# Feed-forward stages of a two-block layer stack on one core: one matmul of 512 columns for two of 256, a residual that is normalized once, and weight splits in halves

## Chip, cores, metric

One NeuronCore of a Trainium2 chip runs the whole program, in one launch. The metric is the device time in microseconds (us), from runs of the same program; lower is better.

## What is computed

Two small transformer blocks behind each other on one sequence of 256 tokens with 1024 channels, in fp32. The first block has a layer with stick-breaking and sparse attention and a layer with forgetting attention, each followed by a feed-forward part with a causal convolution of width 3; the second has a gated linear recurrence and a dilated attention, each with a plain feed-forward part before and behind it. So there are six feed-forward parts, each with 2816 hidden channels:

```python
def rmsnorm(x, g):
    y = x * lax.rsqrt(jnp.mean(x * x, axis=-1, keepdims=True) + NORM_EPS)
    return y * g

def conv_glu_ffn(h, w_in, conv_w, conv_b, w_out):       # first block, twice
    a, b = jnp.split(h @ w_in, 2, axis=-1)
    a = causal_depthwise_conv(a, conv_w) + conv_b
    return (jax.nn.silu(a) * b) @ w_out                 # x = x + that

def _swiglu(h, w_in, w_out):                            # second block, four times
    gate, up = jnp.split(h @ w_in, 2, axis=-1)
    return (jax.nn.silu(gate) * up) @ w_out             # x = x + 0.5 * that
```

with `h = rmsnorm(x, gain)`. Between the blocks the final norm of the first is applied to x, and the first norm of the second follows at once.

## The kernel before

The residual `x` lies transposed in SBUF, channels on the partitions: 8 chunks (KC) of 128 channels by 256 tokens (T). The matrices are products of fp32 numbers made of fp32r matmuls: each operand is split into a high part (`H`, rounded to fp32r) and a low part (`L`, the rest), and a product is three matmuls, H x H, H x L and L x H, added up in PSUM. TensorE (PE) holds 128x128 weights (a weight load, PEld in the trace, goes with each matmul) and streams 256 tokens.

*Weights.* `w` (L266 to L278) fetches a piece of 8 (or 6) chunks by 256 columns, 1 MB, by a DMA that SP issues, into one of two `raw` buffers, and `w_split` (L262 to L264) makes H on ACT (a copy, L263) and L on DVE (a subtraction, L264), by quarters of 512 columns. There are four buffers for the split pieces.

*The residual's operand.* When a chunk of x is final, `done` calls `split_x`: ACT writes xH = x * gain (L328), DVE writes xL = x * gain - xH (L329). The norm's factor R (one number for each token) is not in the operand; it is multiplied in behind the matmul.

*A feed-forward stage* is `ffn` (L447 to L519). `project` makes a piece of two blocks of 128 hidden channels with `gemm`, 48 matmuls (L308 to L310) into one PSUM bank; six banks go round. For m = 0, 2, ..., 20 there is one piece of gate and one of up. `norm` (or `first`, in the third stage) makes R while the first pieces run: squares on ACT, sums on DVE, a matmul with ones over the partitions, then Ln and Exp on ACT and a Newton step on DVE whose last operation is L401. `act` takes the two banks: DVE multiplies by R (L475 or L478 for the gate, L488 for up), the convolution runs on ACT and DVE (L481, L484), Silu on ACT, the product on DVE (L489), and `split` (L313, L314) writes it as hH and hL. The output part goes over four pairs of 128 channels, three weight pieces each; its matmuls (`mm3`, L282 to L284) go into two banks, one for each 128 channels, and one operation on DVE (L516, or L518 with the factor 0.5) adds each to x; then `done` follows.

*Third stage.* `first` makes the factor of the first block's final norm, R1, and from it that of the second block's first norm; it also rewrites x = x * gain * R1, eight operations on DVE (L1448). The product of both factors is what `act` multiplies by.

The order on each engine is set when the program is built, by a list scheduler that goes by priorities and its own estimates of durations; on the chip each engine works its list off in order and waits on semaphores. The stages in order: even (attention), f0, fox (attention), f1, s00, hgrn (recurrence), s01, s10, dilated (attention), s11. In the trace, f0 is the first feed-forward stage and s00 the third.

## Time and profile before

| | |
|---|---|
| median of 3 runs | 1888.78 us (1884.24 to 1891.77) |
| span of the profiled execution | 1880.8 us, 37768 instructions |
| time of that execution beside its span | not listed apart; the three times lie 3.4 to 11.0 us above the span |
| matmuls, weight loads | 15687 each |
| weights read | 311 MB from HBM, 166 GB/s over the span |
| granted clock of TensorE, mean | 0.999 |

The profile is of one execution. PE's busy time is made of modelled ends and counts a matmul from its start to its end, although they overlap; how close it is to its peak is seen from the distances of the starts. A group's line can be that of a helper: all matmuls of `gemm` stand at L308 to L310, whichever stage calls it. A unit of the split is told by its tile (`wH`, `xH`, `hH`).

### The profile page before, as it was taken

The numbers are of one execution on the slowest core, as the hardware profiler recorded it, in microseconds if no ns is written. First come the engines' busy times: TensorE is split into PE (matmuls) and PEld (weight loads), VectorE is DVE, ScalarE is ACT, GpSimd is POOL, SyncE is SP. The second block draws the span as 40 slices with busy tenths as digits, with TensorE's granted clock in tenths as the row PEclk, the third lists the DMA queues.
The fourth block names the chain that finished last, engine by engine and source line by source line (L and its number), as shares of the span: only waits on it lengthen the run. The fifth ranks groups of instructions, "written<-read, shape, count | busy, mean of one in ns | idle before, by whom it ended". The sixth has DMA issues, their size and how long they took to land.

```text
span 1880.8 us, 37768 instructions
## 1 busy us (share of the span) xinstructions
PE 1865.1 (99%) x15687; PEld 1830.0 (97%) x15687; DVE 1271.5 (68%) x2695; ACT 1041.1 (55%) x2167; POOL 3.9 (0%) x18
## 2 busy tenths in 40 slices
PE   8999999999999999999999999999999999999999
PEld 7989999999999999999999999999999999999999
DVE  6557886654888586658998765767566456558662
ACT  5456655455666455445766544645456556556442
POOL 0000000000000000000000000000000000000000
PEclk9999999999999999999999999999999999999999
DMA  7303555541555546455335555555554434326552
GB/s 250 124 32 135 207 196 180 183 152 57 182 218 201 186 165 216 175 185 180 118 107 209 198 192 181 197 185 191 186 204 159 154 130 152 123 90 221 185 195 96
DMA packets 61160, 314.72 MB, mean 167 GB/s; under 512 B 10459, under 2 KB 21115, under 8 KB 28348
## 3 DMA queue, kind: packets, MB, share of 16 engines
...
q8 instruction: 123, 2.02, 0.4%
...
HBM read 311.17 MB, written 1.11 MB: 166 GB/s over the span
## 4 chain that ended last, share of the span: by engine, by line
PE 96%; DVE 2%; DMA 1%; ACT 1%; issue 0%; SPq 0%; ACTq 0%
PE ps_mm L308 21%; PE ps_mm L310 21%; PE ps_mm L309 21%; PE ps_mm L284 7%; PE ps_mm L282 7%; PE ps_mm L283 7%; PE ps_S L317 5%; PE ps_o L317 4%; DMA raw<-in_wall_dram 1%; PE ps_PT L1340 1%; PE ps_PT L317 1%; PE ps_PT L588 1%; DVE wL L264 1%; PE ps_PT L1285 0%; PE ps_PT L614 0%; DVE x L535 0%
## 5 line engine op out<-in xcount | busy, mean ns | idle before, releaser
L263 ACT CAST wH<-raw 128x512 fp32r<-128x512 f32 (+1 forms) x1212 | 651.3, 597 | 525.1 <-PE ps_mm L309 259.9
L264 DVE TENSOR_TENSOR wL<-raw,wH 128x512 fp32r<-128x512 f32 (+1 forms) x1212 | 755.8, 662 | 260.5 <-ACT wH L263 256.8
L308 PE MATMUL ps_mm<-xH,wH 128*128 128x256 f32 x2560 | 717.2, 280 | 8.6 <-ACT xH L328 7.0
L310 PE MATMUL ps_mm<-xH,wL 128*128 128x256 f32 x2560 | 716.1, 280 | 0.2 <-DVE wL L264 0.2
L309 PE MATMUL ps_mm<-xL,wH 128*128 128x256 f32 x2560 | 714.8, 279 | 0.6 <-DVE xL L329 0.4
L308 PEld LDWEIGHTS ps_mm<-xH,wH 128*128 128x128 f32 x2560 | 484.7, 189 | 10.4 <-ACT xH L328 7.0
L309 PEld LDWEIGHTS ps_mm<-xL,wH 128*128 128x128 f32 x2560 | 483.7, 189 | 1.4 <-DVE xL L329 1.3
L310 PEld LDWEIGHTS ps_mm<-xH,wL 128*128 128x128 f32 x2560 | 482.7, 189 | 1.1 <-DVE wL L264 0.7
L284 PE MATMUL ps_mm<-hH,wL 128*128 128x256 f32 x1056 | 297.6, 282 | 0.0
L282 PE MATMUL ps_mm<-hH,wH 128*128 128x256 f32 x1056 | 297.6, 282 | 0.0
L283 PE MATMUL ps_mm<-hL,wH 128*128 128x256 f32 x1056 | 297.5, 282 | 0.0
L283 PEld LDWEIGHTS ps_mm<-hL,wH 128*128 128x128 f32 x1056 | 200.3, 190 | 0.0
L284 PEld LDWEIGHTS ps_mm<-hH,wL 128*128 128x128 f32 x1056 | 200.3, 190 | 0.0
L282 PEld LDWEIGHTS ps_mm<-hH,wH 128*128 128x128 f32 x1056 | 200.3, 190 | 0.0
L308 PE MATMUL ps_mm<-wH,kH 128*128 128x256 f32 x384 | 108.3, 282 | 0.0
L309 PE MATMUL ps_mm<-wL,kH 128*128 128x256 f32 x384 | 107.6, 280 | 0.0
L310 PE MATMUL ps_mm<-wH,kL 128*128 128x256 f32 x384 | 107.5, 280 | 0.0
L308 PE MATMUL ps_mm<-wH,xH 128*128 128x256 f32 x368 | 104.3, 284 | 0.0
L310 PE MATMUL ps_mm<-wH,xL 128*128 128x256 f32 x368 | 103.6, 282 | 0.0
L309 PE MATMUL ps_mm<-wL,xH 128*128 128x256 f32 x368 | 103.4, 281 | 0.0
L488 DVE TENSOR_TENSOR t<-ps_mm,R 128x512 f32<-128x512 f32 x66 | 45.5, 690 | 82.6 <-PE ps_mm L310 82.5
L308 PE MATMUL ps_mm<-oH,wH 128*128 128x256 f32 x256 | 73.4, 287 | 0.0
...
## 6 DMA issues: line engine op xcount, KB each, us to landing
...
```

Of the source, the lines that this page charges most:

```text
L263: self.nc.scalar.copy(H[:, s], raw[:, s])
L264: self.nc.vector.tensor_sub(L[:, s], raw[:, s], H[:, s].bitcast(F32))
L282: nc.tensor.matmul(out, A[0], B[0], start=start, stop=False)
L283: nc.tensor.matmul(out, A[0], B[1], start=False, stop=False)
L284: nc.tensor.matmul(out, A[1], B[0], start=False, stop=stop)
L308: nc.tensor.matmul(out[:, j, :], A[0], B[0], start=c == c0 and j == 0, stop=False, **k)
L309: nc.tensor.matmul(out[:, j, :], A[0], B[1], start=False, stop=False, **k)
L310: nc.tensor.matmul(out[:, j, :], A[1], B[0], start=False, stop=c == c1 - 1, **k)
L317: self.nc.tensor.matmul(out, l, r, start=start, stop=stop, **k)
L488: nc.vector.tensor_mul(t2[:], u, Rb)
L588: nc.tensor.transpose(pp[:, i * P:(i + 1) * P], s, self.ident[:])
L1340: nc.tensor.transpose(pp[:, i], Pt[:, t, i * P:(i + 1) * P], self.ident[:])
```

## The change

In the feed-forward stages alone:

- H and L of an operand lie in one tile (`xB`, `nB`, `hB`, and `wB` for the weights), so that one matmul can stream both: `pair_step` lets the high weights meet [H | L], 512 columns, into a whole bank, and then the low weights meet H, 256 columns, into its first half. Two matmuls and two weight loads where there were three. The sum lies in two halves of a bank, which are added when it is read (`join`: ACT copies the second half out, DVE adds the first; in the output part two additions to x).
- A piece takes two banks (one for each 128 channels), so three pieces share the six banks.
- The operand is normalized once: `normalize` makes nB = split(x * gain * R), two chunks at a time, after the norm. Only the pieces with m < 4 (`EARLY`) still use the raw operand and multiply by R behind it.
- Weight pieces of `nB` and of the output part are split in halves of 1024 columns instead of quarters.

All other changes are names (of tiles, and `gain` as an argument of `ffn`), places of small tiles and comments that are gone; their line numbers move by up to 49. The core of the diff:

```diff
 def w(self, *key):
...
-            for i in range(4):
-                self.w_split(raw, H, L, slice(i * n // 4, (i + 1) * n // 4))
+            q = self.parts
+            for i in range(q):
+                self.w_split(raw, H, L, slice(i * n // q, (i + 1) * n // q))
...
+    def pair(self):
+        t = self.ps.tile([P, 1024], F32, name="ps_pair", tag="pair", bufs=self.tags["pair"] // 2)
+        return t[:].rearrange("p (j h t) -> p j h t", j=2, h=2)
+
+    def pair_step(self, o, WH, WL, XB, first, last):
+        mm, k = self.nc.tensor.matmul, {"skip_group_check": True}
+        mm(o, WH, XB, start=first, stop=False, **k)
+        mm(o[:, 0, :], WL, XB[:, 0, :], start=False, stop=last, **k)
+
+    def gemm_pair(self, o, W, XB):
+        for c in range(KC):
+            for j in range(2):
+                s = slice(j * P, (j + 1) * P)
+                self.pair_step(o[:, j], W[0][:, c, s], W[1][:, c, s], XB[:, :, c, :], c == 0, c == KC - 1)
...
 def ffn(...):
+        EARLY = 4
-            self.banks(ctx, mm=6, sm=2)
+            self.banks(ctx, pair=6, sm=2)
...
             def project(m, n):
-                o = self.psum((P, 2, T))
-                W = self.w(tag, n, m)
-                self.gemm(o, W)
+                self.parts = 4 if m < EARLY else 2
+                o = self.pair()
+                self.gemm_pair(o, self.w(tag, n, m), self.xB if m < EARLY else nB)
+                self.parts = 4
                 return o
+            def normalize(c0, Rx):
+                t = fp.tile([P, 2, T], F32, name="xn", tag="t2")
+                for i in range(2):
+                    c = c0 + i
+                    nc.vector.scalar_tensor_tensor(t[:, i, :], self.x[:, c, :], gain[:, c:c + 1], Rx[:],
+                                                   op0=ALU.mult, op1=ALU.mult)
+                self.split(nB[:, 0, c0:c0 + 2, :], nB[:, 1, c0:c0 + 2, :], t[:])
+
+            def join(dst, o, tmp, early):
+                nc.scalar.copy(tmp, o[:, :, 1, :])
+                if early:
+                    nc.vector.tensor_add(tmp, o[:, :, 0, :], tmp)
+                    nc.vector.tensor_mul(dst, tmp, R[:, None, :].to_broadcast([P, 2, T]))
+                else:
+                    nc.vector.tensor_add(dst, o[:, :, 0, :], tmp)
...
-                    nc.vector.tensor_mul(t1[:], g, Rb)
+                    join(t1[:], g, t1[:], m < EARLY)
...
                 if m == 2:
                     act(0, g, u)
+                    for c in range(0, KC, 2):
+                        normalize(c, Rx)
...
-                            self.mm3(o[j], (W[0][:, c, s], W[1][:, c, s]), (hH[:, k, :], hL[:, k, :]),
-                                     k == 0, k == NF - 1)
+                            self.pair_step(o[:, j], W[0][:, c, s], W[1][:, c, s], hB[:, :, k, :], k == 0, k == NF - 1)
                 for j in range(2):
                     x = self.x[:, m + j, :]
-                    if alpha == 1.0:
-                        nc.vector.tensor_add(x, o[j], x)
+                    for h in (1, 0):
+                        if alpha == 1.0:
+                            nc.vector.tensor_add(x, o[:, j, h, :], x)
...
 def first():
...
-            R = self.sp.tile([P, T], F32, name="R12", bufs=1)
-            self.rsqrt_rows(R[:], m2[:])
-            nc_.vector.tensor_mul(R[:], R[:], R1[:])
+            R2 = self.hp.tile([P, T], F32, name="R2", bufs=1)
+            self.rsqrt_rows(R2[:], m2[:])
+            nc_.vector.tensor_mul(R[:], R2[:], R1[:])
...
-            return R
+            return R, R2
```

How the change moves instructions is seen at three places. The first is PE in stage s00, where the fourth piece ends and the fifth begins (the number behind a tile's name is that of its buffer). Before:

```order
L308 MATMUL ps_mm_8223<-xH_75,wH_8225 128x256
L309 MATMUL ps_mm_8223<-xL_76,wH_8225 128x256
L310 MATMUL ps_mm_8223<-xH_75,wL_8226 128x256
L308 MATMUL ps_mm_8292<-xH_75,wH_8294 128x256
L309 MATMUL ps_mm_8292<-xL_76,wH_8294 128x256
L310 MATMUL ps_mm_8292<-xH_75,wL_8295 128x256
```

and in the changed kernel:

```order
L325 MATMUL ps_pair_6897<-xB_75,wB_6898 128x256
L324 MATMUL ps_pair_6897<-xB_75,wB_6898 128x512
L325 MATMUL ps_pair_6897<-xB_75,wB_6898 128x256
L324 MATMUL ps_pair_6953<-nB_6659,wB_6954 128x512
L325 MATMUL ps_pair_6953<-nB_6659,wB_6954 128x256
L324 MATMUL ps_pair_6953<-nB_6659,wB_6954 128x512
```

Three rows have become two, and the operand changes from `xB` to `nB` at the fifth piece, where it stayed the same before.

The second is DVE in the same stage, from the end of the norm's factor on. Before (R12 is the product of both factors):

```order
L401 TENSOR_TENSOR R12_8137<-R12_8137,rsr_8138 128x256
L264 TENSOR_TENSOR wL_8425<-raw_8423,wH_8424 128x512
L1446 TENSOR_TENSOR R12_8137<-R12_8137,R_8120 128x256
L264 TENSOR_TENSOR wL_8425<-raw_8423,wH_8424 128x512
L475 TENSOR_TENSOR t1_8216<-ps_mm_7960,R12_8137 128x512
L488 TENSOR_TENSOR t2_8215<-ps_mm_8021,R12_8137 128x512
L475 TENSOR_TENSOR t1_8285<-ps_mm_8154,R12_8137 128x512
L488 TENSOR_TENSOR t2_8284<-ps_mm_8223,R12_8137 128x512
L264 TENSOR_TENSOR wL_8486<-raw_8484,wH_8485 128x512
L489 TENSOR_TENSOR t2_8215<-t2_8215,t1_8216 128x512
```

and in the changed kernel (R2 is the second factor alone, `xn` the normalized chunks):

```order
L422 TENSOR_TENSOR R2_6804<-R2_6804,rsr_6805 128x256
L266 TENSOR_TENSOR wB_7044<-raw_7045,wB_7044 128x1024
L1495 TENSOR_TENSOR R12_6803<-R2_6804,R_6786 128x256
L499 SCALAR_TENSOR_TENSOR xn_6877<-x_74,par_71,R2_6804 128x256
L508 TENSOR_TENSOR t1_6866<-t1_6866,R12_6803 128x512
L508 TENSOR_TENSOR t2_6865<-t2_6865,R12_6803 128x512
L499 SCALAR_TENSOR_TENSOR xn_6877<-x_74,par_71,R2_6804 128x256
L499 SCALAR_TENSOR_TENSOR xn_6882<-x_74,par_71,R2_6804 128x256 x2
L508 TENSOR_TENSOR t1_6942<-t1_6942,R12_6803 128x512
L530 TENSOR_TENSOR t2_6865<-t2_6865,t1_6866 128x512
L335 TENSOR_TENSOR nB_6659<-xn_6877,nB_6659 128x512
```

Between the factor and the first two chunks of `nB` (last row) stand one half of a weight split and the products of the early pieces.

The third is PE at the beginning of fox, where the norm's sum over the partitions stands among the first matmuls of that stage. Before:

```order
L310 MATMUL ps_mm_4167<-xH_75,wL_4170 128x256
L308 MATMUL ps_mm_4167<-xH_75,wH_4169 128x256
L309 MATMUL ps_mm_4167<-xL_76,wH_4169 128x256
L317 MATMUL ps_PT_4327<-acc_4314,ones_77 128x256
L310 MATMUL ps_mm_4167<-xH_75,wL_4170 128x256
```

and in the changed kernel:

```order
L312 MATMUL ps_mm_3517<-xB_75,wB_3518 128x256
L313 MATMUL ps_mm_3517<-xB_75,wB_3518 128x256
L311 MATMUL ps_mm_3517<-xB_75,wB_3518 128x256
L338 MATMUL ps_PT_3675<-acc_3662,ones_76 128x256
L312 MATMUL ps_mm_3517<-xB_75,wB_3518 128x256
```

The row with `acc` was the 27th behind the last output matmul of f0 and is now the 20th.

## Rows read from the trace of the kernel before

**Rows 1.** The page of the profile: its part 1 (busy us of each engine, share of the span, instructions) and the first lines of its part 4 (the chain of work that ended last, as shares of the span by engine, then by engine, tile and line).
```profile
PE 1865.1 (99%) x15687; PEld 1830.0 (97%) x15687; DVE 1271.5 (68%) x2695; ACT 1041.1 (55%) x2167; POOL 3.9 (0%) x18
...
PE 96%; DVE 2%; DMA 1%; ACT 1%; issue 0%; SPq 0%; ACTq 0%
...
PE ps_mm L308 21%; PE ps_mm L310 21%; PE ps_mm L309 21%; PE ps_mm L284 7%; PE ps_mm L282 7%; PE ps_mm L283 7%; PE ps_S L317 5%; PE ps_o L317 4%; DMA raw<-in_wall_dram 1%; PE ps_PT L1340 1%; PE ps_PT L317 1%; PE ps_PT L588 1%; DVE wL L264 1%; PE ps_PT L1285 0%; PE ps_PT L614 0%; DVE x L535 0%
```

**Rows 2.** The waits of PE, longest first: who waited <- for whom: us in total, times, longest.
```profile
PE ps_mm L308 <- ACT xH L328: 7.0, 1, 7.0
...
PE ps_PT L317 <- DVE acc L386: 0.5, 1, 0.5
```

**Rows 3.** The busy time of each engine by stretch, for the input and the output stretch of each of the six feed-forward stages (all six input stretches, two of the six output stretches, and the sum over all twelve). Columns: from:to, length, busy us and instructions of PE, PEld, DVE, ACT and POOL, granted clock, share of DMA, GB/s.
```profile
171.40:296.20 124.80, 124.80 (x1058) 124.75 (x1059) 105.09 (x191) 77.14 (x143) 0.00 (x0) 1.00 0.54 193
...
487.60:608.10 120.50, 120.50 (x1061) 120.45 (x1060) 106.00 (x193) 78.23 (x145) 0.17 (x3) 1.00 0.55 200
...
608.10:670.50 62.40, 62.40 (x530) 62.40 (x529) 36.00 (x65) 30.43 (x60) 0.00 (x0) 1.00 0.53 189
...
670.60:795.40 124.80, 124.80 (x1062) 124.69 (x1061) 92.77 (x164) 67.12 (x125) 0.00 (x0) 1.00 0.53 187
...
1002.60:1128.00 125.40, 124.89 (x1066) 122.78 (x1065) 93.39 (x157) 69.19 (x128) 0.00 (x0) 1.00 0.54 196
...
1190.50:1312.70 122.20, 122.20 (x1062) 122.15 (x1061) 87.10 (x148) 66.37 (x123) 0.00 (x0) 1.00 0.53 190
...
1693.20:1813.70 120.50, 120.47 (x1058) 120.44 (x1059) 88.99 (x148) 65.05 (x121) 0.00 (x0) 1.00 0.56 202
...
1813.70:1877.00 63.30, 63.30 (x531) 63.30 (x529) 25.39 (x46) 18.89 (x37) 0.00 (x0) 1.00 0.38 132
...
sum 1114.40, PE 1113.86 PEld 1111.46 DVE 783.27 ACT 593.93 POOL 0.17; mean PE 92.82 PEld 92.62 DVE 65.27 ACT 49.49 POOL 0.01
```

**Rows 4.** The order of time on PE, from a steady input stretch of the second stage. Columns: start us, duration us, instruction.
```profile
520.03 0.28 PE L308 MATMUL ps_mm<-xH,wH 128*128 128x256 f32 x1
520.15 0.28 PE L309 MATMUL ps_mm<-xL,wH 128*128 128x256 f32 x1
```

**Rows 5.** The same on PEld (the weight loads), at the same place.
```profile
520.04 0.19 PEld L309 LDWEIGHTS ps_mm<-xL,wH 128*128 128x128 f32 x1
```

**Rows 6.** The order of time on PE in the attention stages: matmuls with 24, 256, 512 and 128 moving columns (fp32r only in the second row). xN at the end: N in a row, the duration from the start of the first to the end of the last.
```profile
40.64 3.65 PE L317 MATMUL ps_PT<-gw,x 128*128 128x24 f32 x32
...
48.09 0.41 PE L308 MATMUL ps_mm<-xH,wH 128*128 128x256 f32 x1
...
87.75 1.02 PE L317 MATMUL ps_PT<-rp_s,c_rot 128*128 128x512 f32 x2
...
1501.25 0.93 PE L1285 MATMUL ps_PT<-c_ident,qk 128*128 128x128 f32 x7
```

**Rows 7.** The instructions at the tile rp_s: durations in ns, least/median/most.
```profile
L317 PE MATMUL ps_PT<-rp_s,c_rot x6: 592/592/697, 66.9 to 100.8; 128*128 128x512 f32 x6
```

**Rows 8.** The order of time on DVE: the last step of the norm's factor (L401) at the start of each stage (twice in the third), and three runs of equal instructions.
```profile
183.38 0.43 DVE L401 TENSOR_TENSOR R<-R,rsr 128x256 f32<-128x256 f32 x1
...
500.29 0.43 DVE L401 TENSOR_TENSOR R<-R,rsr 128x256 f32<-128x256 f32 x1
...
672.69 0.76 DVE L349 TENSOR_TENSOR acc<-acc,sqg 128x256 f32<-128x256 f32 x2
...
680.03 1.28 DVE L264 TENSOR_TENSOR wL<-raw,wH 128x512 fp32r<-128x512 f32 x2
...
688.32 2.06 DVE L1448 SCALAR_TENSOR_TENSOR x<-x,par,R 128x256 f32<-128x256 f32 x5
...
692.77 0.42 DVE L401 TENSOR_TENSOR R<-R,rsr 128x256 f32<-128x256 f32 x1
...
1018.18 0.43 DVE L401 TENSOR_TENSOR R<-R,rsr 128x256 f32<-128x256 f32 x1
...
1203.35 0.43 DVE L401 TENSOR_TENSOR R<-R,rsr 128x256 f32<-128x256 f32 x1
...
1705.35 0.42 DVE L401 TENSOR_TENSOR R<-R,rsr 128x256 f32<-128x256 f32 x1
```

**Rows 9.** Groups by line, shapes kept apart: line, engine, operation, out<-in, forms, count | busy us, mean ns of one | idle time before them and what ended it.
```profile
L264 DVE TENSOR_TENSOR wL<-raw,wH 128x512 fp32r<-128x512 f32 x1020 | 662.1, 687 | 189.2 <-ACT wH L263 186.0 <-PE ps_mm L310 2.1
...
L264 DVE TENSOR_TENSOR wL<-raw,wH 128x256 fp32r<-128x256 f32 x32 | 11.8, 419 | 0.0
...
L518 DVE SCALAR_TENSOR_TENSOR x<-ps_mm,x 128x256 f32<-128x256 f32 x32 | 13.5, 422 | 24.9 <-PE ps_mm L284 24.9
...
L313 ACT CAST fH<-fr 128x1024 fp32r<-128x1024 f32 x1 | 1.1, 1056 | 0.1
...
L1261 ACT COPY qk<-ps_mm 128x512 f32<-128x512 f32 x24 | 14.1, 587 | 35.9 <-PE ps_mm L310 35.9
```

**Rows 10.** The busy time by stretch (columns as in rows 3) around the first rows of rows 6.
```profile
44.00:50.00 6.00, 6.00 (x35) 5.46 (x35) 3.82 (x8) 3.81 (x8) 0.00 (x0) 0.72 0.53 175
46.00:48.00 2.00, 2.00 (x11) 2.00 (x10) 0.56 (x1) 1.81 (x5) 0.00 (x0) 0.50 0.97 262
```

**Rows 11.** The order of time on PE at the end of the first feed-forward stage: its last output matmul, and the matmul of the norm behind it.
```profile
358.59 0.28 PE L284 MATMUL ps_mm<-hH,wL 128*128 128x256 f32 x1
...
361.72 0.70 PE L317 MATMUL ps_PT<-acc,ones 128*128 128x256 f32 x2
```

52 lines of the change are left out of this document (29 added, 23 removed).

## The prediction

> **What bounds the kernel now.** I read the page's busy shares and chain first. TensorE (PE) is busy 99% of a span of 1880.8 us, and the chain that ended last is 96% PE, most of it at the three matmul lines of `gemm` (L308 to L310) and of `mm3` (L282 to L284) [rows 1]. Then the waits of PE: one of 7.0 us at the start, while the first chunk comes in, and otherwise short ones, such as 0.5 us once for the norm's sum [rows 2]. So no other engine holds PE up; only what PE itself does, or a new wait, can move the time. Third, the busy times by stretch for the six feed-forward stages, two stretches each, twelve in all: 1114.4 us of the span [rows 3]. The code has 1056 matmuls for the inputs and 528 for the outputs of a stage, 9504 in all, so one costs 1114.4 / 9504 = 117.3 ns; 113.6 ns in the best stretches, 120 in the worst.
>
> Why 117 and not less is what decides the change. In a steady stretch matmul follows matmul every 0.11 us, and each weight load starts within 10 ns of the matmul before the one that it serves [rows 4, 5]: one load is hidden under one matmul, and no more. The load has a floor: 32 matmuls with only 24 columns, each with its own load of 128 columns, take 3.65 us, 0.11 us each, though they stream next to nothing [rows 6]. The stream has another price. Seven plain fp32 matmuls of 128 columns take 0.93 us, the last of them some 0.28, so they follow each other in 0.11 us, and two of 512 columns take 1.02 us, of which 0.592 is the last one's own duration [rows 6, 7], so their distance is 0.43 us. That is 0.84 ns per column and a fixed 2 or 3 ns, with the load of 128 columns wholly hidden. The kernel's fp32r matmuls do 256 columns in 113.6 ns, so they stream a column in half that time, and their 256 columns are about 109 ns of stream: less than the load. At 256 columns the load sets the pace; at 512 the stream should.
>
> **The sum, part by part.**
>
> (a) *Two matmuls for three.* Three matmuls of 256 columns, three loads, become one of 512 and one of 256, two loads; columns stay the same. Before: 3 x 117.3 = 352 ns. After: the 512 needs half of the 0.43 us, 216 ns, with the next load under it; the 256 has the load of the next high weights under it and stays load-bound at 117.3. Together 333 ns, 19 ns less, 3168 times: **-59 us**. Bounds: if the 256 falls to 113.6 throughout and the 512 to 213, 327 ns and -79 us; if the 512 also carries the excess that the 256 shows over its pure columns (117.3 - 106.7 = 10.6 ns, so 224), 341 ns and -34 us. I take 216 because the pair of fp32 matmuls is the same number of array steps with the same load beside it, the nearest row there is.
>
> (b) *The new wait: normalized operand.* Only the four pieces with m < 4 still use the raw operand; the fifth asks for `nB`, which needs the norm's factor, then per two chunks two scalar_tensor_tensors, a cast on ACT and a subtraction on DVE. PE reaches it after 4 x 16 x 333 ns = 21.3 us of the stage. When was the factor there before? The stages start at 171.4, 487.6, 670.6, 1002.6, 1190.5 and 1693.2 us [rows 3]; the last step of the factor (L401) ends at 183.8, 500.7, 1018.6, 1203.8 and 1705.8 in the five ordinary ones [rows 8]: 12.4 to 16.0 us in. Behind it the new DVE order has, until the first two chunks of `nB` are written, in the stages with convolution: a product and a join and a product (0.60 each back to back, [rows 8, 9]), two halves of a weight split at 1.14 (0.60 for 512 columns, and 512 more at 1.04 ns), four steps of the convolution and four normalizing steps at 0.395, a product and the subtraction: some 8.5 us. That is 21 to 24 us, against 21.3: the last chunks come another 4 to 5 us later while PE wants them within 4, and the split of the next piece stands behind them in the queue. Up to 3 us for a stage, less where there is no convolution (four DVE steps fewer twice): **+8 us** for five, bounds 0 and 15.
>
> The third stage (`s00`) is different. Its factor comes from two norms in a row, with eight rewrites of x between: R2 is complete at 693.2 us [rows 8], 22.6 us in. After it the order shows a half split 1.14, R12 0.34, four normalizing steps 1.6, three products 1.8, one more product 0.6 and the subtraction 0.7: 6.1 us. First chunks at 28.7 us against 21.3: 7.4 us of wait, and 1.5 more for the last chunks: 9. A long wait has a second price. The one place where the granted clock falls in this trace is after those 32 matmuls of 24 columns: between 46 and 48 us it is 0.50, the lower of its two levels (1.2 GHz of 2.4), a row of a matmul there is 0.41 us long instead of 0.28 [rows 4, 6, 10]; a mean of 0.72 over 6 us means 3.4 us at the lower level, which loses 1.7. If PE stands still for 9 us I expect the same fall: +2. **+11 us**, bounds 6 and 14. The Trainium skill (TensorE: Matmul & The Clock Gate, "HAM oscillation") says the same against this change, that a matmul stream with long enough gaps goes back to half rate; by it every long wait pays this, without it s00's would be 9. No stretch of this trace has such a wait of PE after the start.
>
> (c) *Hand-over to the next stage.* The output sum now lies in two halves of a bank, so each block of the residual takes two additions of 0.42 us (L518, [rows 9]) in series where it was one: 0.34 us more on the way to the norm. In the stage after the first feed-forward the norm's matmul on PE now stands 20 rows behind the last output matmul, 27 before: PE comes to it 0.8 us earlier and its operand 0.34 us later. Before, PE ended the outputs at 358.59, began the norm's matmul at 361.72 and had waited 0.5 us for it [rows 2, 11]. Before hgrn its place is the same, 34 rows behind, and only the later operand counts. 1.2 and 0.3 us, and at each place one part of a weight split (0.60) that may now come between the two additions and the norm's sums: **+3 us**, bounds 0 and 8. At the very end one more addition: **+0.4**.
>
> (d) *Off the path.* Splits in halves: two casts of 1024 columns on ACT (1.056 us each by the one such row, [rows 9]) for four of 512, two subtractions on DVE for four; a join adds a copy out of PSUM (0.587, L1261) and turns a product into a sum. By piece of 5.3 us DVE does 2 x 1.14 of split and about 2 of the rest, ACT 2.1 and 1.5: both stay under PE, as in the stretch with DVE busy 106.0 of 120.5 us [rows 3]. PSUM goes from six banks in turn to three pairs; a pair is read within two pieces, 10 us. If that cover were gone, a late read would stop PE for its own length, a microsecond or two per stage; I count nothing.
>
> Sum: -59 + 8 + 11 + 3 + 0.4 = -36.6, on the profiled span 1880.8 - 36.6 = 1844.2. That execution's span lies 8.0 us under the median of the three times, 1888.78; I leave these 8 as they are: **1852 us**. A measurement of this kernel can tell some 0.5%, 9.4 us, from no change: faster means under 1879.3.
>
> **Rivals.**
>
> 1. *The pair is better still.* Once every second load has 216 ns, the 256 settles at its best 113.6 and the starts are half covered: -71 + 4 + 8 = -59, **1830 us**. For: f1 and s11 hold 113.6 for a whole stretch. Against: the output stretches never do. Chance 0.17.
> 2. *The 512 carries the excess.* -34 + 22.4 = -12, **1877 us**, half of it inside the 0.5%. For: in every stretch a matmul costs 7 to 13 ns more than its columns, and the trace has no 512-column fp32r one. Against: the 0.43 us of fp32. Chance 0.19.
> 3. *The start-of-stage wait eats it all: slower.* One mechanism, at one place: the normalizing steps sit in DVE's queue behind halves of weight splits, each twice as long as the quarters were, so every link of the norm's chain waits longer. It decides once the first chunks of `nB` come 31 us after a stage's start instead of 21 to 24, since six waits of 10 us are 59. With 12 us in the five, 16 in s00 and 3 at the hand-overs: 1888.8 - 59 + 79 = **1909 us**. For: DVE is busy 88% in the stages with convolution. Against: the factor itself is 12 to 16 us in. Chance 0.06.
> 4. *The load alone sets the pace.* If streams overlapped so that only loads counted, two loads would replace three: 3168 x 117.3 = -372 us, and 1888.8 - 372 + 22 = **1540 us**. Against: two fp32 matmuls of 512 columns are 0.43 us apart, not 0.11. Chance 0.01. (The Trainium skill, same page, "Back-to-back issue gap", gives 131 ns sustained for a 512-column matmul in a stream of loads and matmuls, which would come near this; the rows here speak against it.)
>
> **How the numbers follow.** The forecast has 0.57, the rivals 0.17, 0.19, 0.06 and 0.01. Faster by over 0.5%: 0.57 but for a tail of 0.02, 0.17, 0.11 of the second rival, 0.01: 0.84. Within 0.5%: 0.08 of the second and 0.02 of the tail: 0.10. Slower: 0.06. The range takes in the first rival and most of the second, and leaves out its worst, the third and the fourth: **1826 to 1881 us**.
>
> **What would show it.** By stretch: an input stretch with 704 matmuls near 117 us plus its wait, an output stretch with 352 near 58.6. In the timeline: 0.216 us from a 512 to the 256 behind it, 0.113 to 0.12 from there to the next. Among the waits of PE: `nB` from DVE or ACT, about 9 us once and 0 to 3 five times, and the clock at 0.50 behind the long one. It is wrong in (a) if the 512 takes over 224 ns, in (b) if the ordinary waits exceed 4 us or s00's is under 4, and in (d) if PE waits for a pair of banks or for weights in mid-stage.

## The result, and the profile after

The changed kernel takes **1908.01 us** (median of 4 runs, 1905.05 to 1913.74), the kernel before 1888.62 on the same chip: ratio 1.0101, 95% interval [1.0071, 1.0132]. It is slower by 1%, clear of the spread; the forecast was 1852, range 1826 to 1881. The profiled execution of after is the slowest of its four (1913.74, span 1912.0), that of before (span 1880.8) was quicker than its median: the two traces differ by 31.2 us, the medians by 19.4, so the trace overstates the loss.

The page of after, its part 1 and the chain that ended last (for [rows 1]):

```profile
PE 1882.4 (98%) x12519; PEld 1698.0 (89%) x12519; DVE 1315.8 (69%) x2479; ACT 1087.6 (57%) x1963; POOL 3.9 (0%) x18
...
PE 91%; DVE 6%; DMA 1%; ACT 1%; issue 0%; SPq 0%; ACTq 0%; DVEq 0%
PE ps_pair L324 38%; PE ps_pair L325 19%; PE ps_mm L311 7%; PE ps_mm L313 7%; PE ps_mm L312 7%; PE ps_S L338 5%; PE ps_o L338 3%; DVE wB L266 2%; DMA raw<-in_wall_dram 1%; PE ps_PT L1388 1%; PE ps_PT L338 1%; PE ps_PT L636 1%; DVE x L583 0%; DVE xB L350 0%; PE ps_PT L1333 0%
```

PE is still the bound, but PEld fell from 97% to 89%: in the feed-forward stages one load in three is gone (15687 loads became 12519), as the change meant, and the time did not follow. The waits of PE (for [rows 2]; who waited <- for whom: us in total, times, longest):

```profile
PE ps_pair L324 <- DVE nB L335: 7.6, 1, 7.6
...
PE ps_pair L324 <- DVE x L583: 3.4, 4, 1.0
PE ps_PT L338 <- DVE acc L407: 2.4, 2, 2.0
```

There is one wait for `nB` and, in the feed-forward stages, none for a pair of banks or for weights. The busy time by stretch (for [rows 3]): the input and output stretch of f0, the input stretches of f1, s00, s01, s10, s11, and the sum over all twelve. Columns: from:to, length, busy us and instructions of PE, PEld, DVE, ACT and POOL, granted clock, share of DMA, GB/s.

```profile
173.10:297.90 124.80, 124.79 (x706) 108.44 (x707) 110.93 (x165) 85.31 (x125) 0.00 (x0) 1.00 0.54 194
297.90:360.00 62.10, 62.10 (x353) 53.94 (x352) 37.07 (x53) 29.84 (x43) 0.00 (x0) 1.00 0.53 188
492.90:617.80 124.90, 124.86 (x706) 108.45 (x707) 111.15 (x166) 85.66 (x126) 0.00 (x0) 1.00 0.55 194
...
680.00:815.50 135.50, 127.89 (x711) 110.60 (x710) 100.41 (x142) 76.68 (x109) 0.00 (x0) 0.96 0.48 171
...
1025.90:1152.70 126.80, 126.80 (x712) 108.86 (x713) 96.01 (x124) 74.63 (x104) 0.00 (x0) 1.00 0.54 192
...
1214.90:1339.90 125.00, 125.00 (x710) 108.50 (x709) 94.38 (x126) 75.43 (x107) 0.00 (x0) 1.00 0.52 185
...
1720.00:1844.90 124.90, 124.90 (x707) 108.34 (x708) 94.61 (x121) 73.47 (x103) 0.00 (x0) 1.00 0.54 194
...
sum 1134.40, PE 1126.74 PEld 976.49 DVE 817.63 ACT 634.04 POOL 0.00; mean PE 93.90 PEld 81.37 DVE 68.14 ACT 52.84 POOL 0.00
```

The sum is 1134.4 us where it was 1114.4. In before, f0 and s00 took 124.8, but f1 and s11 120.5, s10 122.2; in after, none takes under 124.8. Below, the pace is the distance between the starts of one matmul and the next, and a pair is one matmul of 512 columns with the one of 256 behind it. How a pair is paced shows in the order of time on PE in f1 (for [rows 4]), and on PEld (for [rows 5]; start us, duration us, instruction):

```profile
520.15 0.28 PE L325 MATMUL ps_pair<-nB,wB 128*128 128x256 f32 x1
520.27 0.40 PE L324 MATMUL ps_pair<-nB,wB 128*128 128x512 f32 x1
520.51 0.28 PE L325 MATMUL ps_pair<-nB,wB 128*128 128x256 f32 x1
520.63 0.39 PE L324 MATMUL ps_pair<-nB,wB 128*128 128x512 f32 x1
520.86 0.28 PE L325 MATMUL ps_pair<-nB,wB 128*128 128x256 f32 x1
```

```profile
520.16 0.19 PEld L324 LDWEIGHTS ps_pair<-nB,wB 128*128 128x128 f32 x1
```

From a 512 to the 256 behind it 0.24 us at one pair and 0.23 at the next, where the forecast had 0.216; from the 256 to the next 512, 0.12. Over whole stages a 512 takes 229 to 241 ns (mean 235), a 256 takes 114 to 121 (mean 118.5): the pair is 353.4 ns and was forecast at 333; the three matmuls of before were 340 to 360.

The third stage's wait, on PE and as a window over it (for [rows 10]; at the line's end the idle time before it and who ended it):

```profile
703.64 0.28 PE L325 MATMUL ps_pair<-xB,wB 128*128 128x256 f32 x1
711.51 0.77 PE L324 MATMUL ps_pair<-nB,wB 128*128 128x512 f32 x1 [7.59 <-DVE nB L335]
712.07 0.42 PE L325 MATMUL ps_pair<-nB,wB 128*128 128x256 f32 x1
712.29 0.63 PE L324 MATMUL ps_pair<-nB,wB 128*128 128x512 f32 x1
```

```profile
703.00:715.00 12.00, 4.41 (x17) 3.59 (x16) 12.00 (x24) 8.07 (x11) 0.00 (x0) 0.63 0.23 87
```

7.6 us of wait, then matmuls of 0.63 and 0.42 us in place of 0.40 and 0.28, with a granted clock of 0.63 over 12 us: the lower level, 1.2 GHz of 2.4, for 10.2 us in the trace's clock records, which start inside the wait. The Trainium skill (TensorE: Matmul & The Clock Gate, "HAM oscillation") describes this fall behind a gap, and here the trace agrees. The hand-over behind f0 (for [rows 11]): the last output matmul, and the norm's.

```profile
360.02 0.28 PE L325 MATMUL ps_pair<-hB,wB 128*128 128x256 f32 x1
...
364.43 0.95 PE L338 MATMUL ps_PT<-acc,ones 128*128 128x256 f32 x2 [1.98 <-DVE acc L407]
```

The norm's matmul is 4.4 us behind the last output matmul (3.1 before) and waited 1.98 us (0.5 before); as it began, the clock fell to its lower level for 3.4 us, which before had not happened. It does not follow from the wait alone: e1_widths and e6_poke_after (below) have the same wait of 1.98 us and the same fall, while e2, e3, e10 and e14 wait 1.80 to 1.90 us there and show no fall.

**The 31.2 us by place**, each the difference of the two traces: input stretches that lost a faster pace +13.0 (f1 4.5, s11 4.3, s10 2.8, s01 1.4); s00 +10.6; output stretches -3.5; between the stages +9.9 (ahead of f0 1.8, fox 3.9, hgrn 3.5, dilated 0.7); end +1.2. The 1.8 ahead of f0 is not the change's: at 44 to 47 us the clock is at its lower level for 6.8 us in after and 3.4 in before, and in the traces of the other runs for 0, 3.4 or 6.8 us, with pairs (e3 none, e7 6.8) as with three matmuls (e12 none, e8 6.8).

### The profile page after: what moved, and what is told of

The parts are those of the page before. It is cut to its first block, busy times and chain, and to the rows that moved or that the text cites. A ratio compares the mean times of both kernels' runs of the same rounds, so it can differ in the third digit from the quotient of the medians.

```text
span 1912.0 us, 31020 instructions
## 1 busy us (share of the span) xinstructions
PE 1882.4 (98%) x12519; PEld 1698.0 (89%) x12519; DVE 1315.8 (69%) x2479; ACT 1087.6 (57%) x1963; POOL 3.9 (0%) x18
## 4 chain that ended last, share of the span: by engine, by line
PE 91%; DVE 6%; DMA 1%; ACT 1%; issue 0%; SPq 0%; ACTq 0%; DVEq 0%
PE ps_pair L324 38%; PE ps_pair L325 19%; PE ps_mm L311 7%; PE ps_mm L313 7%; PE ps_mm L312 7%; PE ps_S L338 5%; PE ps_o L338 3%; DVE wB L266 2%; DMA raw<-in_wall_dram 1%; PE ps_PT L1388 1%; PE ps_PT L338 1%; PE ps_PT L636 1%; DVE x L583 0%; DVE xB L350 0%; PE ps_PT L1333 0%
## 5 line engine op out<-in xcount | busy, mean ns | idle before, releaser
L266 DVE TENSOR_TENSOR wB<-raw,wB 128x512 fp32r<-128x512 f32 (+4 forms) x852 | 724.6, 877 | 253.1 <-ACT wB L265 252.3
L265 ACT CAST wB<-raw 128x512 fp32r<-128x512 f32 (+4 forms) x852 | 617.0, 772 | 309.3 <-PE ps_pair L325 159.3
L324 PE MATMUL ps_pair<-nB,wB 128*128 128x512 f32 x1728 | 613.1, 399 | 7.6 <-DVE nB L335 7.6
L325 PE MATMUL ps_pair<-nB,wB 128*128 128x256 f32 x1728 | 486.6, 282 | 0.0
L324 PEld LDWEIGHTS ps_pair<-nB,wB 128*128 128x128 f32 x1728 | 325.6, 188 | 89.0 <-issue 8.3
L324 PE MATMUL ps_pair<-hB,wB 128*128 128x512 f32 x1056 | 373.4, 398 | 0.0
L325 PEld LDWEIGHTS ps_pair<-nB,wB 128*128 128x128 f32 x1728 | 327.0, 189 | 0.1
L325 PE MATMUL ps_pair<-hB,wB 128*128 128x256 f32 x1056 | 297.0, 281 | 0.0
L324 PEld LDWEIGHTS ps_pair<-hB,wB 128*128 128x128 f32 x1056 | 198.3, 188 | 49.3
L325 PEld LDWEIGHTS ps_pair<-hB,wB 128*128 128x128 f32 x1056 | 199.2, 189 | 0.0
L311 PE MATMUL ps_mm<-xB,wB 128*128 128x256 f32 x448 | 128.9, 288 | 7.4 <-ACT xB L349 7.3
L312 PE MATMUL ps_mm<-xB,wB 128*128 128x256 f32 x448 | 127.8, 285 | 0.1
L313 PE MATMUL ps_mm<-xB,wB 128*128 128x256 f32 x448 | 127.4, 284 | 0.0
L311 PE MATMUL ps_mm<-wB,kH 128*128 128x256 f32 x384 | 108.3, 282 | 0.0
L312 PE MATMUL ps_mm<-wB,kH 128*128 128x256 f32 x384 | 107.5, 280 | 0.0
```

Source lines behind the costliest of these rows:

```text
L265: self.nc.scalar.copy(H[:, s], raw[:, s])
L266: self.nc.vector.tensor_sub(L[:, s], raw[:, s], H[:, s].bitcast(F32))
L311: nc.tensor.matmul(out[:, j, :], A[0], B[0], start=c == c0 and j == 0, stop=False, **k)
L312: nc.tensor.matmul(out[:, j, :], A[0], B[1], start=False, stop=False, **k)
L313: nc.tensor.matmul(out[:, j, :], A[1], B[0], start=False, stop=c == c1 - 1, **k)
L324: mm(o, WH, XB, start=first, stop=False, **k)
```

## Experiments

Two theories after the result. **S**: the stream of columns sets the pace, also at 256, and the load was never the bound. **L**, the forecast's: the load paces 256 columns. Below, "difference" is the start of the operand's tile less the start of the weights' tile in SBUF, modulo 512 bytes, read from the built programs. A run without an interval was executed once.

### Stream or load

*e1_widths*, the changed kernel with other shapes in f1 (1900.70 us):

```diff
+        if split: mm(o[:hw, 0, :hc // 2], WH[:, :hw], XB[:, 0, :hc // 2]); ...the same for part 1
+        else:     mm(o[:hw, :, :hc // 2], WH[:, :hw], XB[:, :, :hc // 2])
+        if lc:    mm(o[:lw, 0, :lc], WL[:, :lw], XB[:, 0, :lc])
```

> The changed kernel with the second stage's input projections m = 4 to 20 altered in the six middle chunks of K (outputs of that stage are not the reference's: columns of operand or of weights are left out, and m = 20 multiplies zeros in bf16). Per pair of matmuls (weight columns x operand columns), m = 4: three of 128x256; 6: 128x384 + 128x192; 8: 128x256 + 128x128; 10: 128x128 + 128x64; 12: 64x512 + 64x256; 14: 128x512 + 64x256; 16: three of 64x256; 18: 128x512 alone; 20: bf16 128x512 + 128x256. Theory S (the stream of the moving columns sets the pace, 0.46 ns a column at fp32r, and the weight load is hidden): 353, 265, 177, and then for m = 10 a floor of the load below 2 x 59 if loads are shorter than 59 ns; 353 for m = 12, 14 and 16; 235 for m = 18. Theory L (the forecast's: a load of 128 columns takes 117 ns and paces every matmul of 256 columns or fewer, the stream takes 0.42 ns a column): 352, 160 + 117, 117 + 117, 117 + 117; m = 12: 216 + 108; m = 14: 324 to 333; m = 16: 3 x 108; m = 18: 216. For m = 20, if the excess over 0.42 ns a column belongs to the 4-byte operand, bf16 gives 216 + 108 to 117; if it belongs to every stream, 353 again.

Order of time on PE: bf16, then weights of 64 columns with their loads on PEld, then 256 + 128 columns.

```profile
599.91 0.38 PE L344 MATMUL ps_pair<-bx,bw 128*128 128x512 bf16 x1
600.12 0.27 PE L345 MATMUL ps_pair<-bx,bw 128*128 128x256 bf16 x1
600.23 0.38 PE L344 MATMUL ps_pair<-bx,bw 128*128 128x512 bf16 x1
```

```profile
558.02 0.40 PE L338 MATMUL ps_pair<-nB,wB 128*64 128x512 f32 x1
558.25 0.28 PE L340 MATMUL ps_pair<-nB,wB 128*64 128x256 f32 x1
558.37 0.40 PE L338 MATMUL ps_pair<-nB,wB 128*64 128x512 f32 x1
```

```profile
558.02 0.13 PEld L340 LDWEIGHTS ps_pair<-nB,wB 128*64 128x64 f32 x1
```

```profile
539.70 0.33 PE L338 MATMUL ps_pair<-nB,wB 128*128 128x256 f32 x1
539.87 0.22 PE L340 MATMUL ps_pair<-nB,wB 128*128 128x128 f32 x1
539.92 0.33 PE L338 MATMUL ps_pair<-nB,wB 128*128 128x256 f32 x1
```

Means of the distances over 24 pairs (over 12 where a piece began with a wait), in ns, beside what the theories wanted:

| weight x operand columns | measured | S | L |
|---|---|---|---|
| three of 128x256 | 119 + 118 + 118 = 355 | 353 | 352 |
| 128x384 + 128x192 | 196 + 89 = 285 | 265 | 277 |
| 128x256 + 128x128 | 165 + 58 = 224 | 177 | 234 |
| 128x128 + 128x64 | 136 + 80 = 216 | a floor under 118 | 234 |
| 64x512 + 64x256 | 233 + 117 = 350 | 353 | 324 |
| 128x512 + 64x256 | 229 + 118 = 347 | 353 | 324 to 333 |
| three of 64x256 | 117 + 117 + 117 = 350 | 353 | 324 |
| 128x512 alone | 233 | 235 | 216 |
| bf16 128x512 + 128x256 | 216.8 + 109.0 = 326 | left open: 324 to 333, or 353 | |

At the widths of this kernel the numbers are those of S: with loads of 64 columns, 0.13 us long in the trace instead of 0.19, the pair gets at most 2% shorter (347 is also the faster of two paces that whole pairs show below), and the 512 alone, with the longest cover for a load, still takes 233. At 256 + 128 columns and below, the load binds, which S did not expect so early: these two pairs fit two loads of 128 columns, 112 and 108 ns each, as [rows 6] had it. So S holds here by a thin margin, a load of 108 to 112 ns under a stream of 113 to 120. The pair 384 + 192 fits neither theory, nor two loads; that stays open. In bf16 (zeros, at one place in SBUF) both widths come out where the forecast had them, 216 and 109, so what is dearer seems to belong to fp32r; bf16 at other places was not run. The Trainium skill (TensorE: Matmul & The Clock Gate, "Back-to-back issue gap") gives N/2.4 + 2.5 ns for a matmul of N columns alone. The bf16 distances agree with it; the fp32r ones lie 4 to 12% above it.

*e2_three*, the 512 as two matmuls of 256 with the same weights:

```diff
-        mm(o, WH, XB, start=first, stop=False, **k)
+        mm(o[:, 0, :], WH, XB[:, 0, :], start=first, stop=False, **k)
+        mm(o[:, 1, :], WH, XB[:, 1, :], start=False, stop=False, **k)
```

> The changed kernel with each matmul of 512 columns issued as two of 256 columns with the same weights: three weight loads per step again, all else (pairs of sums, normalization, splits in halves) as changed. Theory S: loads are free, the step stays at 353 ns, 1908 us, 1901 to 1915. Rival: loads do cost, and the change gained by leaving one out but lost the same elsewhere: slower than 1920.

1925.57 us, ratio to before 1.0201 [1.0168, 1.0233]: the rival's side, so S does not hold to the letter. In the trace its input stretches are 0.2 to 2.6 us longer than the change's, its output stretches 0.3 (1.2 in the last two), 11.6 us in all or 3.7 ns a step. Three matmuls at these tiles cost 355 to 360 ns, the pair 353.4. At the places of its own tiles the pair does gain 2 to 7 ns a step; the forecast wanted 19.

### The waits

*e3_raw*, no normalization, and *e7_early8*, more raw pieces in s00 and the last output pair as before (three matmuls and one addition):

```diff
-        EARLY = 4
+        EARLY = NF                                  # e3; normalize() is not called
+        EARLY = 8 if tag == "s00" else 4            # e7
...
+                            if m < KC - 2: self.pair_step(...)      # e7
+                            else: self.mm3(o[:, j, 0, :], ...)
```

> The changed kernel without the normalization: all input projections read the raw operand and every joined sum is multiplied by the norm's factor, as the first two projections of each stage are in the change. Theory S plus wait: the third stage's input stretch falls from 135.5 to about 125 us and its stretch at half clock goes, the other five keep 124.8 to 126.9 (paces of 353 ns), so 1908 - 11 = 1897 us, 1892 to 1902. Rival: the wait at the start of the third stage is for the norm's factor itself and comes back at the next buffer, 1905 or more. By the forecast's term (a), still claimed, no input stretch would be above 117.

> The changed kernel with eight instead of four chunks of the third stage's hidden width read from the raw operand (its normalization has twice the time), and the last pair of output blocks of each stage as three matmuls of 256 columns into one half, added to the residual in one step as before. Expected by the wait theory: the third stage's input stretch 125.5 us instead of 135.5 (-10), and the hand-over to the next stage or head -1 to -3 us in the gaps behind the first and third stage and the end (together -3 to -6): 1908 - 13 = 1895 us, 1890 to 1900. Rival: the hand-over's loss is not from the two additions: 1898 or more, with the gaps at 132.8 and 148.2 as in the change.

e3 took 1899.48 (ratio 1.0068 [1.0047, 1.0090]), e7 1896.90 (1.0059 [1.0038, 1.0080]). The input stretch of s00, in e3 and in e7:

```profile
674.90:800.40 125.50, 125.48 (x710) 108.78 (x709) 105.78 (x183) 78.89 (x141) 0.00 (x0) 1.00 0.52 184
```

```profile
675.40:802.00 126.60, 125.36 (x709) 108.72 (x709) 102.54 (x152) 77.80 (x117) 0.00 (x0) 1.00 0.51 183
```

125.5 and 126.6 instead of 135.5 (in e7 with another wait of 1.2 us, for weights): the wait and its clock were the normalization's. In e7 the gap behind f0 fell from 132.9 to 130.0 us (before 129.0), the one behind s00 from 148.3 to 146.1 (before 144.8). In e3, which keeps both additions and shows no fall of the clock there, they are 131.6 and 148.4. So of the 5 us that e7 gave back there, some 4 go to the second addition and the rest to the clock. Both runs end 8 to 11 us under the change (6 to 8 by their ratios to before, each on its own chip) and still above before; what is left lies mostly in the pace. In e3 all input pieces read the raw operand, at the difference of 448 (below) that before has too, and no input stretch is under 124.8; f1, which before did in 120.5:

```profile
487.90:612.80 124.90, 124.89 (x707) 108.55 (x708) 117.73 (x207) 86.17 (x158) 0.00 (x0) 1.00 0.54 193
```

### A second pace

*e4_poke*, *e5_poke_o* (kernel before) and *e6_poke_after* (changed kernel) put small unused matmuls between the pieces (e4 1894.21 us, e6 1928.53):

```diff
+                if n == "g" and m >= 4: self.poke(m, W)   # e.g. mm(p[:, 0:1], self.par[:, :P], self.ones[:])
                 self.gemm(o, W)
```

> The kernel before, with one or two small matmuls put ahead of the gate projection of m = 4 to 18 in each of the six stages (fp32 128 weight columns x 1, 2 x 1, 8, 64 or 128 moving columns; fp32r x 256, 128 or 64 columns), their result unused; the output stays the reference's. Theory M (the distance of 113.3, 117.8 or 120 ns between equal matmuls is a phase that the matmuls fall into at a restart and keep): the distance steps between these values at some of the 48 places, 10 or more, and stays until the next place. Rival A (addresses of operands or banks set it): the first and third stage keep 117.8 through, the second and last 113.3 through, as without the small matmuls. Whichever form always leads to 113.3 would be worth (117.8 - 113.3) x 1056 = 4.8 us a stage.

> The kernel before, with a small fp32 matmul of 64 moving columns (result unused) ahead of the gate projections m = 4 and 12 of each stage, and one or two small ones ahead of each of the four pairs of output blocks: first and fifth stage fp32 x 64 columns, second and last two fp32 x 1, third fp32r x 64, fourth one fp32 x 1. Theory M (a phase, set by what the matmuls restart behind): in the run of the small matmuls, fp32 x 64 and two fp32 x 1 led to 113.3 ns in all six stages, so the input stretches behind m = 4 go at 113.3: the first and third stage 120.9 to 121.3 us instead of 124.9, the fourth and fifth 121 to 122, the second and last 120.7; the output stretches go to 113.3 (60 us) where the phase can be moved there too. 1888 - 10 = 1878 us with the input stretches alone, 1865 if the outputs follow. Rival A (operands set the distance in the output stretches): these stay at 118.3 and 120.0, 62.4 and 63.3 us, plus 0.1 us for each small matmul.

> The changed kernel with small unused matmuls ahead of the gate projections m = 4 to 20 (first, third and fifth stage the list of the earlier run: fp32 x 1, two x 1, fp32r x 256, 128, 64, fp32 x 8, 64, 128, 64; the others fp32 x 64, 32, two x 1, 16, 96, fp32r x 192, 32, fp32 x 4, two x 1) and one or two ahead of each pair of output blocks. Theory M: the pair of 512 and 256 columns has a faster phase as the triple does, 3 x 113.3 = 340 ns, and some of the small matmuls lead to it; then the change itself would be neutral in pace and only lost the phase. Rival: pairs are at 353.4 whatever comes ahead (each 512 at 229 to 240), so the change took the faster phase away for good: about 13 us in the profile of before.

Three windows of f0 in e4: behind nothing new, behind two fp32 x 1 and an fp32r x 256, and behind one fp32r x 128.

```profile
182.00:192.00 10.00, 10.00 (x87) 10.00 (x86) 9.09 (x18) 8.23 (x16) 0.00 (x0) 1.00 0.50 179
218.00:228.00 10.00, 10.00 (x90) 10.00 (x89) 9.47 (x18) 6.51 (x12) 0.00 (x0) 1.00 0.65 248
229.00:239.00 10.00, 10.00 (x87) 10.00 (x86) 8.55 (x16) 6.04 (x12) 0.00 (x0) 1.00 0.62 211
```

10 us hold 87 matmuls, then 90, then 87: the pace stepped from 117.8 to 113.3 ns and back, each time at a small matmul, and held until the next one. Behind two fp32 x 1 and behind fp32r x 256 all six stages were at 113.3, behind fp32r x 128 all at 117.8 but s10, where two transposes came between. Behind the first, one fp32 x 1, the stages differed: f0, f1 and s11 stepped to 113.3, s01 to 117.8, s00 and s10 stayed. So there are two paces for the same instructions, and a small matmul ahead of them can switch from one to the other. The trace of before has such a step too: in f1 and s11 the first 74 matmuls go at 117.8, and those behind the norm's matmul at 113.3. No form chose reliably: in e5 fp32 x 64 led from the slower to the faster pace (f0, m = 4), back from the faster (f0, m = 12), and at s00's m = 4 nowhere; 1895.32 us, 1.0038 [1.0004, 1.0072], where 1878 or less was expected. e5's output stretches kept 118.3 and 120.0 behind every small matmul. In e6 the pair was at 353.5 ns, and for some pieces at 346.5 (behind fp32r x 128 in f0, x 32 in f1, most pieces of s11). So the pair has two paces as well, but the rival holds where it counts: 340, three times 113.3, never came.

### Where the tiles lie

Before, the output stretches took 62.4 us in four stages and 63.3 in two, with the same code. Tile starts differ there by 32 bytes modulo 64. *e8_w64*, *e9_all64*, *e10_after64* and *e11_x64* move starts with 32 spare bytes:

```diff
+        t = pool.tile([P, 8], F32, name=f"skip{self.pads8}", bufs=1)   # ahead of x, raw or hH
```

> The kernel before, with a tile of 32 bytes a partition put behind the constants, so that the weight tiles (raw, wH, wL) start at a multiple of 64 bytes; in the program before they start at 32 past one, and so do the residual's xH and xL, which stay there. The hidden tiles hH and hL stand at 32 past in the first two stages, at a multiple of 64 in the other four (before: a multiple of 64 in the first four, 32 past in the last two, which are the ones with 118.3 and 120.0 ns in their output stretches). Theory A (a read of 4-byte rows that start off a multiple of 64 bytes costs the matrix engine extra, for weights and operand alike): all distances fall, input stretches to at most 116 us, output stretches of the last four stages to 57.6 us (109 ns, the distance that bf16 had), those of the first two between; 1888 - 50 = 1838 us, 1815 to 1865. Theory M (only a phase that restarts decide): nothing below 113.3 ns, 1870 to 1895.

> The kernel before, with weights, residual (x, xH, xL) and hidden tiles of all six stages at multiples of 64 bytes. Theory A: 109 ns everywhere in the feed-forward stages, input 1056 x 109 = 115.1 us, output 57.6 us: 1888 - 47 - 30 = 1811 us, 1795 to 1835. Theory M: as in the run with the weights alone, 1870 to 1895.

> The changed kernel, with weights, residual, normalized residual and hidden tiles of all stages at multiples of 64 bytes. Theory A: the pair at 217 + 109 = 326 ns as in bf16, input 114.8 us (the third stage 125 with its wait), output 57.4 us: 1908 - 61 - 30 = 1817 us, 1800 to 1840, so still no faster than the kernel before with the same starts. The forecast's premise, rescued (aligned, the stream of 512 takes 216 and the load paces 256 columns at 117): 333 ns, and the kernel before with the same starts stays at 117 a matmul, so the change would gain there. Theory M: 1895 to 1915.

> The kernel before, with residual and hidden tiles at multiples of 64 bytes and the weight tiles still at 32 past. If the weights' start matters alone: as before, 1880 to 1895. If the operand's start matters alone: input stretches at 115 us, output stretches of the last two stages at 62.4 like the first four, 1840 to 1855. If each counts: between this and the run with all three.

1908.58 (1.0122 [1.0095, 1.0150]), 1890.76 (1.0020 [0.9999, 1.0040]), 1907.20 (1.0111 [1.0081, 1.0140]), 1905.83 (1.0103 [1.0075, 1.0132]). Theory A fell: aligned tiles gained nothing, and moving only one side, the weights (e8) or the operands (e11), lost 18 to 21 us. What the output stretches of the four three-matmul programs had in common was the difference: 224 always 118.3 ns, 256 always 120.0, 288 (two stages of e11) 116.8; in input stretches 448 gave 113.3 or 117.8, 416 gave 117.3 to 120. Theory **D**: the difference sets the pace. *e12_sweep* (1914.56 us), *e13_sweep* (1891.69) and *e14_sweep_after* (1909.59) run through it, a value for each stage:

```diff
+            self.skip(hp, {"f0": 9, "f1": 10, "s00": 11, ...}[tag])     # times 32 bytes, ahead of hH (hB)
             hH = hp.tile([P, NF, T], F32R, name="hH")
```

> The kernel before, with spare bytes ahead of tiles, so that the start of the operand less the start of the weights, modulo 512 bytes, is 0 for the residual's parts and 0, 32, 64, 96, 128, 160 for the hidden parts of the six stages in order. Theory D (the distance of the matmuls depends on this difference): the runs so far had 224 -> 118.3, 256 -> 120.0, 288 -> 116.8 ns in output stretches, whatever each start was by itself, and 448 -> 113.3 or 117.8, 416 -> 117.3 to 120 in input stretches. So the six output stretches (62.5 us at 118.3) come out at several paces between 109 and 120 ns, 57.6 to 63.4 us, each steady through its stage. Rival: the differences of the earlier runs were chance, all stretches 62.4 to 63.4.

> The same with 320 for the residual and 192, 320, 352, 384, 448, 480 for the hidden parts. Theory D: as before, several paces; 448 gives 113.3 or 117.8 in an output stretch as it did in input stretches (59.8 or 62.2 us), 192 and 320, the neighbours of 224 and 288, 116 to 120.

> The changed kernel with 0 for the residual and 0, 64, 128, 320, 384, 448 for the normalized residual and the hidden parts of the six stages in order. Theory D for the pair: at differences where the three matmuls are fast the pair is fast in the same ratio (353.4 ns at 224, 256 and 448 so far, which is 3 x 117.8), down to 326 ns, 57.4 us for an output stretch, if one has no conflict at all. Rival: pairs stay at 346 to 353 at every difference, and the change is tied to the slower pace.

Output stretches (528 matmuls) of e12 at 0, 32, 128 and 160, then of e13 at 192, 352 and 448:

```profile
299.20:362.30 63.10, 63.10 (x528) 63.10 (x527) 37.09 (x67) 30.33 (x60) 0.00 (x0) 1.00 0.52 188
620.90:682.90 62.00, 62.00 (x528) 62.00 (x528) 35.81 (x65) 30.18 (x60) 0.00 (x0) 1.00 0.53 191
1338.80:1401.30 62.50, 62.50 (x529) 62.50 (x528) 37.10 (x67) 30.46 (x59) 0.00 (x0) 1.00 0.50 183
1847.00:1908.60 61.60, 61.60 (x527) 61.60 (x526) 25.38 (x46) 18.90 (x37) 0.00 (x0) 1.00 0.39 131
```

```profile
298.50:358.20 59.70, 59.70 (x529) 59.70 (x528) 36.96 (x67) 30.52 (x60) 0.00 (x0) 1.00 0.56 197
800.00:863.20 63.20, 63.20 (x529) 63.20 (x529) 37.09 (x67) 30.29 (x59) 0.00 (x0) 1.00 0.52 181
1323.00:1382.60 59.60, 59.60 (x528) 59.60 (x527) 36.82 (x67) 30.43 (x59) 0.00 (x0) 1.00 0.53 192
```

59.6 to 63.2 us for the same work. All values measured in output stretches, ns per matmul of 256 columns:

| difference | 0 | 32 | 64 | 96 | 128 | 160 | 192 | 224 |
|---|---|---|---|---|---|---|---|---|
| ns | 120.0 | 117.7 | 117.7 | 120.0 | 118.7 | 117.3 | 113.3 | 118.3 |
| difference + 256 | 256 | 288 | 320 | 352 | 384 | 416 | 448 | 480 |
| ns | 120.0 | 116.8 | 117.7 | 120.0 | 118.7 | not run | 113.3, 117.8 | 118.2 |

The two halves agree within 1 ns, so it repeats every 256 bytes, with one good place, 192 and 448. Before, the residual stands at 448, the hidden tiles at 224 and 256. In the change the early pieces still read the residual at 448, but `nB`, behind the hidden tiles, stands at 224 and 256 like them: at these places three matmuls would take 355 or 360 ns (e2). The pair in e14, output stretches of f0, f1 and s11 at 0, 64 and 448 (352 matmuls, 176 pairs):

```profile
298.00:359.90 61.90, 61.90 (x352) 53.72 (x352) 37.05 (x53) 29.75 (x42) 0.00 (x0) 1.00 0.53 187
617.70:679.00 61.30, 61.30 (x353) 53.69 (x352) 35.86 (x51) 29.64 (x43) 0.00 (x0) 1.00 0.54 190
1840.60:1902.50 61.90, 61.90 (x353) 53.74 (x352) 25.98 (x33) 17.71 (x20) 0.00 (x0) 1.00 0.36 132
```

Over all stages the pair took 346.5 to 354 ns, and 353.5 at 448, where three matmuls take 340 at the faster of their paces. The pair is 2 to 7 ns better than three matmuls at the differences where both ran, but for the best one, where it is 13 worse. Its two paces show in e10, whose hidden tiles all stand at 256: the output stretches of s00 and of s10, 347 and 353.5 ns a pair by the distances of the starts.

```profile
811.40:872.30 60.90, 60.90 (x353) 53.69 (x352) 37.05 (x53) 28.54 (x41) 0.00 (x0) 1.00 0.54 191
1332.30:1394.30 62.00, 62.00 (x352) 53.73 (x352) 37.05 (x53) 28.65 (x41) 0.00 (x0) 1.00 0.52 187
```

### Versions

*e15_h448*: before, hidden tiles at 448 (192 or 224 spare bytes ahead of `hH`). *e16_blocks*: with it, the chunks of one block of 128 columns before those of the other. *e17_after_best*: e7 with normalized and hidden parts at 64.

```diff
+            self.skip(hp, {"f0": 7, "f1": 7, "s00": 7, "s01": 7, "s10": 6, "s11": 6}[tag])   # e15, e16
+        for c, j in sorted(order, key=lambda v: v[1]) if blocks else order:                  # e16
```

> The kernel before, with 224 or 192 spare bytes a partition ahead of the hidden tiles of each stage, so that their start less that of the weights is 448 modulo 512 (before: 224 and 256); nothing else. Theory D: output stretches at 113.3 ns, 59.8 us instead of 62.4 (four stages) and 63.3 (two), together -17; input stretches unchanged (120 to 125 us, each with the faster or slower of its two paces, so +-4): 1887 - 17 = 1870 us, 1863 to 1878.

> The same, and from the third pair of projections of each stage on (m of 2 and more) the eight chunks of K of one block of 128 columns before those of the other, as the output stretches have it. If the slower pace of the input stretches at this difference, 117.8 instead of 113.3, belongs to the alternation of blocks: all input stretches at 120.3 to 121 us, another -13: 1857 us, 1850 to 1865. If it is a phase that any order can fall into: as the run without this, within 5 us.

> The changed kernel with what the runs showed for it: normalized residual and hidden parts at the difference of 64 (pairs at 349 ns instead of 353.4), eight early chunks in the third stage, and the last pair of output blocks in three matmuls and one addition. Output stretches 61.4 us, input 123 to 124 (the third 125): 1897 for the last two alone, less 4.4 ns x 2784 pairs = 12, so 1885 us, 1878 to 1892; not below the kernel before with its hidden tiles moved.

e15 takes **1874.24 us** (12 runs), before 1883.92 (23 runs) on that chip: 0.9953 [0.9934, 0.9973], the fastest of all here; a few spare bytes give half a per cent. The gain is 10 us, where 17 were expected, and in its trace two of the six output stretches stayed at the slower pace. Input and output stretch of f0 and of f1:

```profile
171.20:295.70 124.50, 124.48 (x1058) 124.45 (x1059) 105.27 (x191) 77.05 (x143) 0.00 (x0) 1.00 0.53 193
295.80:357.90 62.10, 62.10 (x530) 62.10 (x529) 37.18 (x67) 30.47 (x60) 0.00 (x0) 1.00 0.53 190
487.10:607.50 120.40, 120.40 (x1060) 120.35 (x1059) 105.63 (x193) 78.27 (x145) 0.25 (x4) 1.00 0.56 200
607.60:667.30 59.70, 59.70 (x530) 59.70 (x528) 35.89 (x65) 30.43 (x60) 0.00 (x0) 1.00 0.56 198
```

f1 has both at 113.3 (120.4 and 59.7), f0 both at 117.8 behind its first pieces: at 448 the output stretches have the two paces too, and four of the six took the faster. e16 (1876.57, 0.9960 [0.9940, 0.9980]) had three output stretches and, behind their first pieces, two whole input stretches at the faster one: the order of blocks does not choose it. e17 missed its forecast: 1895.25 (1.0067 [1.0044, 1.0090]); at 64 its pairs went at 353.4, only s01 at 349 in part: the slower of the pair's paces had come in. No form of the pair that was run came below the kernel before.

## Why the prediction was wrong

- **(a) Two matmuls for three: the step that failed.** Forecast -59 us, measured +9.5 in the twelve stretches (the sum's +20.0 less s00's 10.6). The sentence at fault is "less than the load": the forecast put the fp32r stream of 256 columns at 109 ns, by halving fp32's 0.43 us for 512, and read the rest up to 117 as the load. No row of before showed an fp32r matmul of 512 columns, or what 256 take with a shorter load. The load is 108 to 112 ns and hidden; the stream itself takes 113.3 to 120, and at 512 columns 229 to 241 (mean 235, not 216), over the 224 that the forecast named as its sign of being wrong here. A load taken away from under it gave back 2 to 7 ns a step (e2), not 19. The second rival had the mechanism, an excess that the 512 carries, but at the size of one matmul's excess (224); it carries two. By the pace that f1 and s11 held, [rows 3], the forecast did see that the pace varied with the load unchanged, and took the best of it for a better covered load.
- The change also put f1, s11 and parts of s01 and s10 from 340 to 353.4 ns a step: +13.0 us that no term had. It gained 3.5 in the output stretches, where the tiles were at 224 and 256 before and after. Together these make up the +9.5.
- **(b) The wait for `nB`.** s00: forecast +11 (9 of wait, 2 of clock), measured +10.6 (7.6 and about 3): right in mechanism, and the close sum in part luck, as one part came out smaller and the other larger. The five ordinary stages: forecast +8, measured no wait; the bound of 0 was the value.
- **(c) Hand-overs.** Forecast +3.4, measured 11.1 over all gaps and the end, beyond its bound of 8: right in mechanism, a third of the size. Behind f0 it was 3.9: the operand kept PE waiting 1.5 us longer (forecast 1.2), and the clock fell for 3.4 us, which costs 1.7 and did not happen in every run. Behind s00 it was 3.5, of which PE idled 2.6 more than before (forecast 0.3). Ahead of f0 the clock stood at its lower level for 6.8 us instead of 3.4, 1.7 us, which came and went with the execution. At the start of four stages the first 512 waited 3.4 us in all for the addition to x ahead of its operand (1.3 before); it needs both parts of a chunk where the first 256 needed one, which would explain it but was not tried.
- **(d) Splits, joins, PSUM: nothing.** Right: no wait in mid-stage.
- **Rival 3** gave 1909 and the time came out at 1908, but not by its mechanism: it wanted 12 us of wait in each of five stages, and there was none: the agreement is luck.
- **Open.** What in the chip makes the difference of starts count, what chooses between the two paces, and why the pair never reached 340 ns. The spread of e15's times (1866 to 1882) would fit stages that take one or the other from execution to execution; only one execution of each program has a trace, so that is argued, not shown.
